# Storing the last block of a matrix product in pieces of 16, 8 and 8 rows, with two instead of six buffers for the transposed chunks

## Chip, cores, metric

One core of one Trainium2 chip. The metric is the device time of one execution in microseconds (us), as the median of several runs; less is better. PE is the engine for matrix products (PEld its loads of weights), DVE the vector engine, ACT the scalar engine, POOL the general one, and SP here only issues DMAs; SBUF and PSUM are the core's two memories on the chip. Every large DMA is spread over the core's sixteen DMA engines. The profile's span is about 1.8 us shorter than that time (165.4 against 167.18 us for the profiled run before).

## The reference

The reference builds a weight from a matrix, a low-rank product and a norm per column, and multiplies a large x by it. The weight is small; x and the result are 33.5 MB each.

```python
batch, seq_len, in_dim, out_dim = 16, 2048, 256, 256     # rank 16
W_adapted = W + scale * (lora_A @ lora_B)
W_final = W_adapted / np.sqrt(np.sum(W_adapted**2, axis=0, keepdims=True) + 1e-8) * m
y = x.reshape(-1, in_dim) @ W_final                       # 32768 x 256 by 256 x 256
```

## The kernel before

x is cut into 8 blocks of 4096 rows (4 MB), 32 rows per partition. A block is loaded by one DMA on SP's queue, worked on in 8 chunks of 4 rows per partition, overwritten in place with its result, and stored by one DMA on ACT's queue. A chunk goes through four steps: 8 transposes on PE into PSUM, a cast to bf16 on DVE (which moves it to SBUF), 8 products on PE, and a copy from PSUM back into the block on ACT. There are five block buffers, so loads 5, 6 and 7 wait for stores 0, 1 and 2. The order of the instructions on each engine is not the order of the source: the framework's scheduler picks it, and the number of buffers limits it.

```python
J = 4; DJ = 32; BLK = DJ * P; NBLK = N // BLK
xpool  = ctx.enter_context(tc.tile_pool(name="xpool", bufs=5))
xtpool = ctx.enter_context(tc.tile_pool(name="xtpool", bufs=6))
pp_xt  = ctx.enter_context(tc.tile_pool(name="pp_xt", bufs=2, space=bass.MemoryType.PSUM))
pp_y   = ctx.enter_context(tc.tile_pool(name="pp_y", bufs=2, space=bass.MemoryType.PSUM))
# ... (loads of the small inputs, w_final) ...
for b in range(NBLK):
    x_sb = load_x(b)                                   # one nc.sync.dma_start, 4 MB
    for c in range(DJ // J):
        xt_ps = pp_xt.tile([P, KC, J * P], FP32, tag="psxt", name="xt_ps")
        # ... 8 x nc.tensor.transpose into xt_ps ...
        xt_sb = xtpool.tile([P, KC, J * P], BF16, name="xt_sb")
        nc.vector.tensor_copy(out=xt_sb, in_=xt_ps)
        y_ps = pp_y.tile([P, J, OUT], FP32, tag="psy", name="y_ps")
        # ... 8 x nc.tensor.matmul of xt_sb with w_final into y_ps ...
        nc.scalar.copy(out=x_sb[:, c * J : (c + 1) * J, :], in_=y_ps)
    nc.scalar.dma_start(
        out=out_flat[b * BLK : (b + 1) * BLK].rearrange("(p j) k -> p j k", p=P),
        in_=x_sb)
```

Of the kernel before, what the change touches and what calls it, by code (L numbers as in the profile page):

```python
# [11 lines left out]
def kernel(  # L12
# [10 lines left out]
    nc = tc.nc  # L23
    P = 128
# [6 lines left out]
    out_flat = out.flatten_outer_dims()  # L31
# [4 lines left out]
    J = 4  # L36
    DJ = 32
    BLK = DJ * P
    NBLK = N // BLK
# [3 lines left out]
    consts = ctx.enter_context(tc.tile_pool(name="consts", bufs=1))  # L43
    startup = ctx.enter_context(tc.tile_pool(name="startup", bufs=1))
    xpool = ctx.enter_context(tc.tile_pool(name="xpool", bufs=5))
    xtpool = ctx.enter_context(tc.tile_pool(name="xtpool", bufs=6))
    pp_xt = ctx.enter_context(tc.tile_pool(name="pp_xt", bufs=2, space=bass.MemoryType.PSUM))
    pp_y = ctx.enter_context(tc.tile_pool(name="pp_y", bufs=2, space=bass.MemoryType.PSUM))

    def load_x(b):  # L50
        t = xpool.tile([P, DJ, IN], FP32, name="x_sb", tag="x_sb")
        nc.sync.dma_start(
            out=t,
            in_=x_flat[b * BLK : (b + 1) * BLK].rearrange("(p j) k -> p j k", p=P),
        )
        return t
# [23 lines left out]
    with tc.high_priority():  # L80
# [15 lines left out]
        for c in range(KC):  # L96
# [10 lines left out]
            out=wa, in0=ab_ps, scalar=float(scale), in1=w_nat, op0=ALU.mult, op1=ALU.add  # L107
# [21 lines left out]
    for a in range(J // 2):  # L129
        j_order.append(a)  # L130
        j_order.append(a + J // 2)

    for b in range(NBLK):
        x_sb = load_x(b)


        for c in range(DJ // J):
            xt_ps = pp_xt.tile([P, KC, J * P], FP32, tag="psxt", name="xt_ps")
            for j in range(J):
                for kc in range(KC):  # L140
                    nc.tensor.transpose(  # L141
                        xt_ps[:, kc, j * P : (j + 1) * P],
                        x_sb[:, c * J + j, kc * P : (kc + 1) * P],
                        identity,
# [5 lines that stand above are left out]
            for kc in range(KC):  # L150
                for j in j_order:
                    nc.tensor.matmul(  # L152
                        y_ps[:, j, :],
                        xt_sb[:, kc, j * P : (j + 1) * P],
                        w_final[:, kc, :],
                        start=(kc == 0 and (j % (J // 2)) == 0),
                        stop=(kc == KC - 1 and (j % (J // 2)) == (J // 2) - 1),
                    )
            nc.scalar.copy(out=x_sb[:, c * J : (c + 1) * J, :], in_=y_ps)  # L159

        nc.scalar.dma_start(
            out=out_flat[b * BLK : (b + 1) * BLK].rearrange("(p j) k -> p j k", p=P),
            in_=x_sb,
        )


# [33 lines left out]
```

## Time and profile before

| | before |
|---|---|
| median time, 4 runs (range) | 167.03 us (166.91 to 167.78) |
| span of the profiled run | 165.4 us |
| bytes moved | 67.55 MB |
| last copy of a result ends | 153.14 us |
| last store issued | 153.18 us |
| last data packet lands | 163.93 us |

From the page, the span in 40 slices of 4.1 us: busy tenths of PE and of the DMA queues, and the rate.

```profile
PE   0059588888999889988998999888998699797000
...
DMA  6999989899999989999999998989999999992885
GB/s 194 480 412 404 483 380 503 380 380 380 452 432 388 499 380 456 430 404 468 384 491 388 452 432 388 499 382 456 428 404 468 396 471 404 444 444 83 380 380 254
```

The one slice in which the DMA queues are mostly idle is the fourth from the end, where the rate is 83 GB/s. A slice books a packet where it starts, so single slices swing; longer stretches swing less. From the windows of the profile, with for each stretch its length, the busy time of the engines, the granted clock, the busy share of the DMA queues and the rate (x133 means 133 instructions):

```profile
core 0: us, PE busy (x) PEld busy (x) DVE busy (x) ACT busy (x) POOL busy (x), PEclk, DMA share, GB/s
128.00:146.00 18.00, 15.54 (x133) 13.30 (x132) 8.78 (x9) 9.02 (x9) 0.00 (x0) 1.00 1.00 429
...
149.00:151.50 2.50, 2.32 (x21) 1.87 (x20) 0.00 (x0) 2.29 (x3) 0.00 (x0) 1.00 0.33 138
151.50:154.00 2.50, 0.60 (x6) 0.29 (x3) 0.00 (x0) 1.44 (x2) 0.00 (x0) 1.00 0.00 0
154.00:159.00 5.00, 0.00 (x0) 0.00 (x0) 0.00 (x0) 0.00 (x0) 0.00 (x0) 0.59 1.15 492
```

The queues are full (429 GB/s) until about 149 us, start nothing between 151.5 and 154 us, and then work alone. The hole is the wait for the last copy. The timeline of ACT (start, duration, what, and in brackets the idle time before) shows the copy and the store that follows it:

```profile
150.00 1.93 ACT L159 COPY x_sb<-y_ps 128x1024 f32<-128x1024 f32 x2 [0.21 <-PE y_ps L152]
152.13 1.01 ACT L159 COPY x_sb<-y_ps 128x1024 f32<-128x1024 f32 x1 [0.21 <-PE y_ps L152]
153.18 0.34 ACTq L161 DMA_DIRECT2D out_dram<-x_sb  x1
```

The timeline of DVE, from block 0 to block 2, shows how six buffers are used: up to six casts in a row, then a long pause while PE makes the products that belong to them.

```profile
33.40 2.36 DVE L147 CAST xt_sb<-xt_ps 128x1024 bf16<-128x1024 f32 x2 [1.75 <-PE xt_ps L141]
37.51 7.18 DVE L147 CAST xt_sb<-xt_ps 128x1024 bf16<-128x1024 f32 x6 [1.76 <-PE xt_ps L141]
46.75 2.36 DVE L147 CAST xt_sb<-xt_ps 128x1024 bf16<-128x1024 f32 x2 [2.06 <-PE y_ps L152]
54.46 7.18 DVE L147 CAST xt_sb<-xt_ps 128x1024 bf16<-128x1024 f32 x6 [5.36 <-PE xt_ps L141]
```

The trace also holds each DMA packet's start, duration, queue and size. A store ends with one small record of completion per DMA engine; the sixteen of each store say when each of the sixteen engines was done. Sorted, in us:

```
store of block 6:  149.52 149.55 149.56 149.56 149.71 149.97 150.57 150.63 150.76 150.80 150.86 150.95 151.06 151.06 151.10 152.20
store of block 7:  163.76 163.77 163.78 163.78 163.79 163.79 163.81 163.83 163.83 163.84 163.85 163.86 163.87 163.88 163.89 163.92
```

One engine is 1.1 us behind the next and 2.7 us behind the first when block 6 ends. ("The slow engine" is this one of the sixteen.) Its 32 KB packets take 1.27 us in this stretch (18 of them from 129.47 to 152.21 us); 1.213 us is the usual duration, found in 1571 of the 2048. The trace does not name the engine of a packet: "this engine" means packets each of which starts when the one before ends. After the hole all sixteen start level and end level.

### The profile page before, as it was taken

The page shows a single profiled execution, that of the slowest core. Times are in us where ns is not written, and L with a number is a line of the kernel's source. Part 1 is how long each engine was busy: PE and PEld are TensorE (multiplying, and loading weights), DVE is VectorE, ACT ScalarE, POOL GpSimd, SP SyncE. Part 2 cuts the span into 40 slices and gives each one's busy share as a digit, 9 for nine tenths or more (in the row PEclk, how much of TensorE's full clock was granted, in tenths as well). Part 3 has the DMA queues.
Part 4 walks back from the last instruction along what each step waited for, and adds up shares of the span by engine and source line. Part 5 has one row for each costly group of instructions (what it writes and reads, how often), then busy time and mean ns, then how long its engine had stood idle before and what let it go on. Part 6 is the DMA issues. An engine that isn't in the chain of part 4 may idle for free.

```text
span 165.4 us, 2364 instructions
## 1 busy us (share of the span) xinstructions
PE 128.5 (78%) x1034; PEld 107.4 (65%) x1034; DVE 81.3 (49%) x76; ACT 65.6 (40%) x67; POOL 0.7 (0%) x6
## 2 busy tenths in 40 slices
PE   0059588888999889988998999888998699797000
PEld 0037577776788778876877778777786678685000
DVE  0155655559750885059553951577519350780000
ACT  3001244441068405960097039620780089329000
POOL 1000000000000000000000000000000000000000
PEclk9999999999999999999999999999999999999755
DMA  6999989899999989999999998989999999992885
GB/s 194 480 412 404 483 380 503 380 380 380 452 432 388 499 380 456 430 404 468 384 491 388 452 432 388 499 382 456 428 404 468 396 471 404 444 444 83 380 380 254
DMA packets 2892, 67.55 MB, mean 408 GB/s; under 512 B 561, under 2 KB 834, under 8 KB 834
## 3 DMA queue, kind: packets, MB, share of 16 engines
q1 hardware_dynamic: 1424, 33.82, 48.4%
q10 hardware_dynamic: 1458, 33.59, 47.4%
q8 instruction: 8, 0.13, 0.3%
q14 instruction: 2, 0.02, 0.0%
HBM read 33.85 MB, written 33.55 MB: 408 GB/s over the span
## 4 chain that ended last, share of the span: by engine, by line
PE 57%; DVE 23%; ACT 6%; DMA 4%; issue 2%; ACTq 1%
PE y_ps L152 32%; PE xt_ps L141 23%; DVE xt_sb L147 20%; ACT x_sb L159 6%; DMA m_row<-in_m_dram 4%; PE n_ps L115 1%; DVE rnorm L124 1%; PE mb_ps L91 1%; DVE w_final L126 0%; DVE sq L110 0%; DVE wa L106 0%; ACTq L60 0%; ACTq L64 0%; ACT norm L119 0%; PE ab_ps L97 0%
## 5 line engine op out<-in xcount | busy, mean ns | idle before, releaser
L147 DVE CAST xt_sb<-xt_ps 128x1024 bf16<-128x1024 f32 x64 | 75.6, 1220 | 55.7 <-PE xt_ps L141 41.8
L159 ACT COPY x_sb<-y_ps 128x1024 f32<-128x1024 f32 x64 | 63.6, 1014 | 75.1 <-PE y_ps L152 72.8
L141 PE MATMUL xt_ps<-identity,x_sb 128*128 128x128 f32 x512 | 70.6, 278 | 7.0 <-DVE xt_sb L147 6.4
L152 PE MATMUL y_ps<-w_final,xt_sb 128*128 128x256 bf16 x512 | 64.7, 272 | 6.9 <-DVE xt_sb L147 5.0
L141 PEld LDWEIGHTS xt_ps<-identity,x_sb 128*128 128x128 f32 x512 | 57.2, 142 | 15.8 <-DVE xt_sb L147 14.8
L152 PEld LDWEIGHTS <-xt_sb 128*128 128x128 bf16 x512 | 49.1, 97 | 17.4 <-DVE xt_sb L147 6.9
L119 ACT ACTIVATE norm<-n_ps,eps_col 128x256 f32<-128x256 f32 x1 | 0.5, 474 | 10.1 <-PE n_ps L115 10.1
L91 PE MATMUL mb_ps<-m_row,ones 1*128 1x256 f32 x2 | 1.2, 694 | 4.2 <-DMA m_row<-in_m_dram 4.2
L86 PE MATMUL aT_ps<-identity,a_nat 128*16 128x128 f32 x2 | 0.6, 396 | 3.9 <-DMA a_nat<-in_lora_A_dram 3.9
L91 PEld LDWEIGHTS mb_ps<-m_row,ones 1*128 1x128 f32 x2 | 0.5, 304 | 4.7 <-issue 4.7
L115 PE MATMUL n_ps<-sq,ones 128*128 128x256 f32 x4 | 2.1, 674 | 1.5 <-DVE sq L110 1.5
L82 DVE CAST b_bf<-b_nat 16x256 bf16<-16x256 f32 x1 | 0.3, 282 | 5.5 <-DMA b_nat<-in_lora_B_dram 5.5
L124 DVE RECIPROCAL rnorm<-norm 128x256 f32<-128x256 f32 x1 | 1.8, 1753 | 2.0 <-ACT norm L119 2.0
L86 PEld LDWEIGHTS aT_ps<-identity,a_nat 128*16 128x16 f32 x2 | 0.1, 88 | 3.9 <-issue 3.9
L115 PEld LDWEIGHTS n_ps<-sq,ones 128*128 128x128 f32 x4 | 1.2, 324 | 2.2 <-DVE sq L110 2.0
L76 ACT ACT_TABLE_LOAD x1 | 1.3, 1283 | 2.3 <-issue 2.3
L93 DVE COPY m_all<-mb_ps 128x256 f32<-128x256 f32 x1 | 0.4, 425 | 2.9 <-PE mb_ps L91 2.9
L126 DVE TENSOR_TENSOR w_final<-wam,rnorm 128x256 bf16<-128x256 f32 x2 | 0.8, 422 | 0.0
L122 DVE TENSOR_TENSOR wam<-wa,m_all 128x256 f32<-128x256 f32 x2 | 0.8, 416 | 0.0
L110 DVE TENSOR_TENSOR sq<-wa 128x512 f32<-128x512 f32 x1 | 0.7, 692 | 0.0
L106 DVE SCALAR_TENSOR_TENSOR wa<-ab_ps,w_nat 128x512 f32<-128x512 f32 x1 | 0.7, 692 | 0.0
L97 PE MATMUL ab_ps<-b_bf,aT 16*128 16x256 bf16 x2 | 0.6, 416 | 0.0
(11 smaller groups left out, 2.0 us busy)
## 6 DMA issues: line engine op xcount, KB each, us to landing
x_sb<-in_x_dram SPq DMA_DIRECT2D x8, 4096.0 KB, 32.5
out_dram<-x_sb ACTq DMA_DIRECT2D x8, 4096.0 KB, 25.0
w_nat<-in_W_dram SPq DMA_DIRECT2D x1, 256.0 KB, 2.9
a_nat<-in_lora_A_dram ACTq DMA_DIRECT2D x1, 16.0 KB, 3.1
b_nat<-in_lora_B_dram ACTq DMA_DIRECT2D x1, 16.0 KB, 5.2
m_row<-in_m_dram ACTq DMA_DIRECT2D x1, 1.0 KB
```

What stands on the lines that cost most here:

```text
L76: nc.scalar.activation(out=warm, in_=eps_col, func=AF.Sqrt)
L86: nc.tensor.transpose(aT_ps[:, c * P : (c + 1) * P], a_nat[:, c, :], identity)
L91: nc.tensor.matmul(mb_ps, ones[0:1, :], m_row, start=True, stop=True)
L106: nc.vector.scalar_tensor_tensor(out=wa, in0=ab_ps, scalar=float(scale), in1=w_nat, op0=ALU.mult, op1=ALU.add)
L115: nc.tensor.matmul(n2_ps, ones, sq[:, c, :], start=(c == 0), stop=(c == KC - 1))
L122: nc.vector.tensor_mul(out=wam[:, c], in0=wa[:, c], in1=m_all)
L124: nc.vector.reciprocal(out=rnorm, in_=norm)
L126: nc.vector.tensor_mul(out=w_final[:, c], in0=wam[:, c], in1=rnorm)
L141: nc.tensor.transpose(xt_ps[:, kc, j * P : (j + 1) * P], x_sb[:, c * J + j, kc * P : (kc + 1) * P], identity,)
L147: nc.vector.tensor_copy(out=xt_sb, in_=xt_ps)
L152: nc.tensor.matmul(y_ps[:, j, :], xt_sb[:, kc, j * P : (j + 1) * P], w_final[:, kc, :], start=(kc == 0 and (j % (J // 2)) == 0), stop=(kc ...
L159: nc.scalar.copy(out=x_sb[:, c * J : (c + 1) * J, :], in_=y_ps)
```

## The change

The first part keeps the transposes from running ahead of the products, so that a block's result is finished more evenly. The second lets the store of the last block begin after half of it is done, so that little is left to store after the last copy.

```diff
-    xtpool = ctx.enter_context(tc.tile_pool(name="xtpool", bufs=6))
+    xtpool = ctx.enter_context(tc.tile_pool(name="xtpool", bufs=2))
...
+    CH = DJ // J
+    store_after = [[CH] for _ in range(NBLK)]
+    store_after[-1] = [CH // 2, 3 * CH // 4, CH]
...
         x_sb = load_x(b)
+        j_stored = 0
...
             nc.scalar.copy(out=x_sb[:, c * J : (c + 1) * J, :], in_=y_ps)
-        nc.scalar.dma_start(
-            out=out_flat[b * BLK : (b + 1) * BLK].rearrange("(p j) k -> p j k", p=P),
-            in_=x_sb)
+            if c + 1 in store_after[b]:
+                j0 = j_stored
+                j_stored = (c + 1) * J
+                nc.scalar.dma_start(
+                    out=out_flat[b * BLK : (b + 1) * BLK].rearrange(
+                        "(p j) k -> p j k", p=P)[:, j0:j_stored, :],
+                    in_=x_sb[:, j0:j_stored, :])
```

More of the change, by code (lines that the diff above doesn't have):

```diff
@@ L159 @@
             nc.scalar.copy(out=x_sb[:, c * J : (c + 1) * J, :], in_=y_ps)
-        nc.scalar.dma_start(
-            out=out_flat[b * BLK : (b + 1) * BLK].rearrange("(p j) k -> p j k", p=P),
-            in_=x_sb,
-        )
+            if c + 1 in store_after[b]:
[3 more added lines that the diff above has]
+                    out=out_flat[b * BLK : (b + 1) * BLK].rearrange(
+                        "(p j) k -> p j k", p=P
+                    )[:, j0:j_stored, :],
+                    in_=x_sb[:, j0:j_stored, :],
+                )
 _INS = ['x', 'W', 'lora_A', 'lora_B', 'm', 'scale']
```

## The prediction

> **What bounds the kernel now.** By windows of 20 us, from 40 to 140 us the DMA queues move 428 to 434 GB/s. The Trainium skill, page "DMA: Bandwidth & Descriptors", section "Specifications", gives a fabric ceiling of 435 GB/s; this trace agrees (best stretch 434). 67.55 MB at 432 GB/s is 156 us of a 165.4 us span: the body is DMA-bound. Compute hardly waits for loads (0.6 us in the waits), but is nearly as long: chunks run from 17 to 153.1 us, 64 chunks at 2.13 us.
>
> The exception is the tail. The packet records show the store of block 6 running dry between 149.5 and 152.2 us, engine by engine; the timeline shows the last store issued at 153.18 us, after the last copy; its first packet moves at 154.02 us. Then 4.19 MB go alone until 163.93 us. The hole is about 3.7 us of all engines' time. The sixteen engines do not end together: fifteen end block 6 by 151.1 us, one at 152.21 us, because its 32 KB packets took about 1265 ns where the others took 1213. The hole hides that skew: after it all start level and end within 0.17 us.
>
> **What the change does.** Two buffers stop the transposes from running six chunks ahead. In the timeline, blocks 1 to 7 show bursts of six casts (DVE-limited, 1.22 us each) and then bursts of copies; block 0 shows a pair pattern, two transposes then two products, at 4.11 us a pair, which never has more than two transposed chunks alive. I expect that pattern throughout: 16.4 us a block instead of 17, the last copy at about 149 us.
>
> The split adds two DMA issues on ACT (0.34 us each) and makes the last packets 16 or 8 KB. The first 16 rows should be ready at about 141 us (148.9 us even in the old order), before the store queue runs dry at 149.5 us. So the hole closes, and the queues run without a break.
>
> **On the critical path.** Loads and earlier stores do not move: the stores are backlogged, so issuing them earlier changes nothing. What can be won is the hole only: 3.7 us on average over engines, but the end is that of the slowest engine. It ends block 6 at 152.21 us and then has 8 partitions of 32 KB, 9.75 us: 161.96 us instead of 163.93, a gain of 2.0 us; if its lag is smaller in unprofiled runs, up to 3.5 us. Smaller packets and two more completions should cost about 0.1 us (estimate from the 9 ns completion records). I predict 164.7 us; 163.4 to 165.7 should hold it 8 times in 10. Faster by over 2% (under 163.65): 0.2; within 2%: 0.78; slower: 0.02.
>
> **What would show it.** GB/s near 430 in all slices after 146 us; data ending at about 162 us, with a ragged finish of 1 to 2.5 us between engines; the last copy at 147 to 151 us; copies in pairs, 2.05 us a chunk, no burst of six casts; PE and DVE busy times unchanged; the first piece issued before 149 us; the chain of waits ending in DMA.
>
> **What would make it wrong.** An instruction order that with two buffers serialises transpose, cast and product (over 2.3 us a chunk): then block 6's store comes after the queue is dry (142 us) and the gain is lost or reversed. A smaller skew: over 2% faster. Small packets much slower than 32 KB ones: less gain.

## The result

| | before | after |
|---|---|---|
| median time, 4 runs each (range) | 167.03 us (166.91 to 167.78) | 165.17 us (165.07 to 165.55) |
| span of the profiled run | 165.4 us | 163.3 us |
| last copy ends | 153.14 us | 151.29 us |
| last store issued | 153.18 us | 151.33 us |
| last data packet lands | 163.93 us | 161.87 us |
| a block, from store issue to store issue | 17.0 us (blocks 0 to 7, mean) | 16.76 us |

The ratio is 0.988, with an interval of 0.985 to 0.992: within 2%, and clearly not nothing. A ratio here is the mean time of one kernel's fast runs over the mean of the other's of the same rounds, so it is not quite the ratio of the medians.

The slices of the page after: from the second slice on the DMA row stays at 8 or 9 until the last one, and the slice of 83 GB/s is gone.

```profile
PE   0049888888888888888888888898889888886000
...
DMA  6999998999999899999999999999999999999992
GB/s 197 414 474 401 449 450 381 474 425 377 389 425 474 385 470 425 387 482 409 421 466 393 458 429 393 492 393 421 474 401 441 429 409 466 409 413 429 407 425 86
```

The windows after, for the stretches shown of before: no stretch without DMA until 159 us, then a thin end.

```profile
core 0: us, PE busy (x) PEld busy (x) DVE busy (x) ACT busy (x) POOL busy (x), PEclk, DMA share, GB/s
128.00:146.00 18.00, 16.18 (x142) 14.22 (x140) 9.70 (x9) 8.96 (x9) 0.00 (x0) 1.00 0.99 426
...
149.00:151.50 2.50, 1.16 (x10) 0.70 (x8) 0.14 (x1) 2.02 (x2) 0.00 (x0) 1.00 0.95 406
151.50:154.00 2.50, 0.00 (x0) 0.00 (x0) 0.00 (x0) 0.00 (x0) 0.00 (x0) 1.00 1.04 446
154.00:159.00 5.00, 0.00 (x0) 0.00 (x0) 0.00 (x0) 0.00 (x0) 0.00 (x0) 0.56 0.95 401
159.00:162.00 3.00, 0.00 (x0) 0.00 (x0) 0.00 (x0) 0.00 (x0) 0.00 (x0) 0.50 0.36 150
```

The timeline of ACT after: the three pieces are issued at 145.05, 149.16 and 151.33 us.

```profile
145.05 0.34 ACTq L170 DMA_DIRECT2D out_dram<-x_sb  x1
...
149.16 0.34 ACTq L170 DMA_DIRECT2D out_dram<-x_sb  x1
150.28 1.01 ACT L165 COPY x_sb<-y_ps 128x1024 f32<-128x1024 f32 x1
151.33 0.34 ACTq L170 DMA_DIRECT2D out_dram<-x_sb  x1
```

The timeline of DVE after: never more than two casts in a row, in all eight blocks.

```profile
33.61 2.35 DVE L153 CAST xt_sb<-xt_ps 128x1024 bf16<-128x1024 f32 x2 [1.76 <-PE xt_ps L147]
37.72 2.36 DVE L153 CAST xt_sb<-xt_ps 128x1024 bf16<-128x1024 f32 x2 [1.76 <-PE xt_ps L147]
42.14 2.36 DVE L153 CAST xt_sb<-xt_ps 128x1024 bf16<-128x1024 f32 x2 [2.06 <-PE y_ps L158]
46.25 2.36 DVE L153 CAST xt_sb<-xt_ps 128x1024 bf16<-128x1024 f32 x2 [1.76 <-PE xt_ps L147]
```

And the completion records of the sixteen engines, from the packets of the trace:

```
store of block 6:  149.35 149.38 149.44 149.54 149.69 150.22 150.28 150.61 150.73 150.77 150.85 150.88 150.90 150.92 150.94 152.10
last piece:        159.12 159.15 159.20 159.31 159.46 159.99 160.05 160.38 160.50 160.54 160.62 160.65 160.67 160.68 160.70 161.86
```

(The slow engine's record of the piece before, 159.41 us, falls between them and is left out.) The store of block 6 ends where it ended before, engine by engine. The slow engine is done with block 6 at 152.10 us, and then has 8 packets of 16 KB (607 ns each, 4.86 us) and 16 of 8 KB (306 ns each, 4.90 us): 152.10 + 4.86 + 4.90 = 161.86 us, to the hundredth what was recorded. Fifteen engines are done by 160.70 us.

### The profile page after: what moved, and what is told of

It reads as the page before. It is cut to its first block, busy times and chain, and to the rows that moved or that the text cites. A ratio compares the mean times of both kernels' runs of the same rounds, so it can differ in the third digit from the quotient of the medians.

```text
span 163.3 us, 2370 instructions
## 1 busy us (share of the span) xinstructions
PE 125.4 (77%) x1034; PEld 107.9 (66%) x1034; DVE 81.1 (50%) x76; ACT 66.1 (40%) x67; POOL 0.7 (0%) x6
## 4 chain that ended last, share of the span: by engine, by line
PE 57%; DVE 26%; DMA 4%; issue 2%; ACT 1%; DVEq 1%; ACTq 1%
PE y_ps L158 33%; DVE xt_sb L153 23%; PE xt_ps L147 22%; DMA m_row<-in_m_dram 4%; PE n_ps L115 1%; DVE rnorm L124 1%; DVEq L206 1%; PE mb_ps L91 1%; ACT x_sb L165 1%; DVE w_final L126 0%; DVE sq L110 0%; DVE wa L106 0%; ACTq L60 0%; ACTq L64 0%; ACT norm L119 0%
## 5 line engine op out<-in xcount | busy, mean ns | idle before, releaser
L158 PE MATMUL y_ps<-w_final,xt_sb 128*128 128x256 bf16 x512 | 65.5, 273 | 11.5 <-DVE xt_sb L153 11.5
L147 PE MATMUL xt_ps<-identity,x_sb 128*128 128x128 f32 x512 | 68.7, 279 | 3.4 <-DVE xt_sb L153 3.1
L147 PEld LDWEIGHTS xt_ps<-identity,x_sb 128*128 128x128 f32 x512 | 58.7, 144 | 7.8 <-DVE xt_sb L153 6.7
L158 PEld LDWEIGHTS <-xt_sb 128*128 128x128 bf16 x512 | 47.8, 98 | 22.8 <-DVE xt_sb L153 18.2
```

What stands on the lines that cost most here:

```text
L147: nc.tensor.transpose(xt_ps[:, kc, j * P : (j + 1) * P], x_sb[:, c * J + j, kc * P : (kc + 1) * P], identity,)
L158: nc.tensor.matmul(y_ps[:, j, :], xt_sb[:, kc, j * P : (j + 1) * P], w_final[:, kc, :], start=(kc == 0 and (j % (J // 2)) == 0), stop=(kc ...
```

## The experiments

Theories, as they stood before the runs. **A**: the DMA queues set the end, and among the sixteen engines the slowest one: the change is worth just the idle time that this one engine had in the hole, 1.8 us (152.20 to 154.03 us), and not the 3.6 us that the engines had on average (mean start 154.08 less mean end 150.50 us; the prediction says 3.7). **B**: the instruction order earned it; the last copy came 1.85 us earlier and the time fell by 1.86 us, so the numbers of the result alone cannot tell B from A. **C**: the split earned it. **D**: no single engine matters, all sixteen share one rate and the bytes set the end.

| run | median us (range) | ratio to before, interval | last store issued | data end |
|---|---|---|---|---|
| the whole change | 165.17 (165.07 to 165.55) | 0.988 (0.985 to 0.992) | 151.33 | 161.87 |
| e1: split alone | 165.61 (165.16 to 166.97) | 0.990 (0.986 to 0.995) | 153.68 | 162.09 |
| e2: two buffers alone | 165.38 (165.31 to 165.45) | 0.987 (0.983 to 0.992) | 151.38 | 162.13 |
| e3: two pieces of 16 rows | 165.25 (165.13 to 165.28) | 0.987 (0.983 to 0.990) | 151.07 | 161.97 |
| e4: last piece as 120 + 8 partitions | 165.46 (165.30 to 166.09) | 0.989 (0.985 to 0.992) | 151.42 | 162.43 |
| e5: no PE work (wrong) | 162.86 (162.73 to 162.96) | 0.972 (0.967 to 0.977) | 147.58 | 159.85 |
| e6: last stores on SP's queue | 165.17 (164.95 to 165.32) | 0.986 (0.982 to 0.989) | 151.49 | 162.12 |
| e7: four buffers alone | 165.96 (165.06 to 166.94) | 0.990 (0.986 to 0.995) | 151.00 | 161.76 |
| e8: last piece as 80 + 35 + 13 | 166.52 (166.08 to 166.81) | 0.996 (0.994 to 0.998) | 150.98 | 163.01 |
| e9: no PE work, but casts (wrong) | 163.30 (163.24 to 163.57) | 0.977 (0.974 to 0.980) | 145.02 | 160.23 |

Issue and data end are of the profiled run of each kernel; in e4 and e8, where the last piece is two or three DMAs, the issue is that of the first. The kernel before, run beside them, had medians of 167.33, 167.47 and 167.32 us over 11, 11 and 12 runs; one run of each was slow and is left out of the ratios. The edits are given against the changed kernel, shortened where "..." or a comment stands. "Time" in the texts is the median; "queue" in them means one of the sixteen DMA engines' queues.

### e1, the split alone

```diff
-    xtpool = ... bufs=2
+    xtpool = ... bufs=6
```

> Six buffers, last block in three pieces (the split alone). Theory A (the end is set by the slowest DMA queue, busy without a break): the first piece is issued at about 148.9 us, when most queues are about to run dry and the slowest still has 3 us of work, so the data end at about 162 us and the time is 165.2 us (165.0 to 165.6), as with the whole change, although the last copy stays at 153.1 us. Theory B (the instruction order earns it: the last copy came 1.85 us earlier, 151.3 instead of 153.1 us, and the time fell by 1.86 us): this kernel keeps the old order and stays at 166.6 to 167.0 us.

Measured 165.61 us. Here the last copy is even later than before, 153.65 us, because the issues of the first two pieces (0.34 us each) stand between the copies; the data end at 162.09 us all the same. B, as the only cause, falls: the old order with the split earns nearly all of the gain. The timeline of ACT shows the pieces:

```profile
149.00 0.34 ACTq L170 DMA_DIRECT2D out_dram<-x_sb  x1
...
151.34 0.34 ACTq L170 DMA_DIRECT2D out_dram<-x_sb  x1
...
153.68 0.34 ACTq L170 DMA_DIRECT2D out_dram<-x_sb  x1
```

The first piece comes just in time (149.00 us, when the first engines run dry at 149.65 us). The windows show the hole nearly closed:

```profile
149.00:151.50 2.50, 2.08 (x18) 1.67 (x18) 0.00 (x0) 1.93 (x2) 0.00 (x0) 1.00 0.82 341
151.50:154.00 2.50, 0.90 (x8) 0.56 (x6) 0.00 (x0) 1.93 (x2) 0.00 (x0) 1.00 0.98 419
```

Two of the six runs were slower, 166.65 and 166.97 us. They left no trace, so what made them slower stays open.

### e2, two buffers alone

```diff
-    store_after[-1] = [CH // 2, 3 * CH // 4, CH]
```

> Two buffers, last block stored whole (the order alone). Theory A: the hole in the DMA stays but is shorter, the last store is issued at about 151.3 us, its first packets move at 152.1 us on all queues together, and 9.9 us later, at 162.0 us, the data end level (spread under 0.3 us): 165.2 us (165.0 to 165.6). So each part alone would earn nearly all, and the two together no more. Theory B: 165.2 us too. Theory C (the split earns it all): 167.0 us.

Measured 165.38 us, data end 162.13 us, with the sixteen engines level within 0.15 us (161.97 to 162.12). C, as the only cause, falls. This is the run that is most worth looking at, because the hole is still there. Its windows, and the issue of its one store of the last block:

```profile
146.00:149.00 3.00, 2.55 (x24) 2.13 (x21) 2.16 (x2) 1.12 (x2) 0.00 (x0) 1.00 0.89 382
149.00:151.50 2.50, 1.22 (x10) 0.70 (x8) 0.20 (x1) 2.02 (x2) 0.00 (x0) 1.00 0.34 144
151.50:154.00 2.50, 0.00 (x0) 0.00 (x0) 0.00 (x0) 0.00 (x0) 0.00 (x0) 0.85 0.98 419
...
151.38 0.34 ACTq L169 DMA_DIRECT2D out_dram<-x_sb  x1
```

Fifteen engines run dry between 149.2 and 151.2 us and are idle until about 152.2 us, and it costs next to nothing, because the slow engine is busy with block 6 until 152.05 us, and the last store, issued at 151.38 us, reaches the engines at about 152.2 us. The whole change closes this hole for the fifteen too, and its data end only 0.26 us earlier (161.87 us): idle time of fifteen engines was next to free as long as the sixteenth had almost none.

By itself e2 cannot tell A from B. Its store is issued 1.80 us earlier than before, and its data end 1.80 us earlier; that this shift is just the idle time of the slow engine (1.8 us) is chance.

So each half of the change earns almost the whole gain, and the two together no more: 1.7 us (e1, by medians), 1.95 us (e2) and 1.86 us (both).

### e3, two pieces of 16 rows

```diff
-    store_after[-1] = [CH // 2, 3 * CH // 4, CH]
+    store_after[-1] = [CH // 2, CH]
```

> Two buffers, last block in two pieces of 16 rows. Theory A: the last piece is issued at about 151.3 us while the queues have work until 154.2 us, so the third piece is not needed: 165.2 us, within 0.2 us of the whole change, with the same ragged end. Rival (a small last piece shortens the tail): 165.7 us or more.

Measured 165.25 us, data end 161.97 us, with the slow engine last again (161.96 us, the others by 161.17 us). The third piece earns nothing: the second of two pieces is issued at 151.07 us, and the engines have work until 154.24 us.

### e4, one engine without a share of the last piece

```diff
-                nc.scalar.dma_start(out=...[:, j0:j_stored, :], in_=x_sb[:, j0:j_stored, :])
+                # last piece only: cuts = [0, P - 8, P], else [0, P]
+                for p0, p1 in zip(cuts[:-1], cuts[1:]):
+                    nc.scalar.dma_start(out=...[p0:p1, j0:j_stored, :], in_=x_sb[p0:p1, j0:j_stored, :])
```

> The whole change, but the last piece of 8 rows goes as two DMAs: partitions 0 to 119 (15 queues of 8 partitions) and 120 to 127 (8 queues of one partition), so that one of the sixteen queues has nothing of the last piece. Theory A, if the slowest queue is the one left out: its 8 packets of 306 ns are gone, the others get 0.3 us at most, the data end at about 161.0 us instead of 161.9: 164.3 us (164.0 to 164.6). If the slowest is another queue: 165.1 to 165.6 us, and the page of the packets tells whether it carried 8 or 9 of them. Theory D (all queues share one rate, 432 GB/s, and the raggedness is noise): 165.2 us.

Measured 165.46 us. This run rests on a statement of the Trainium skill, page "DMA: Bandwidth & Descriptors", section "Why a DMA increments its semaphore by 16 and not by 1": a DMA from SP or ACT uses the lowest-numbered k engines, k being the largest number up to 16 that divides the slowest dimension of both sides. The trace agrees in that the 120-partition piece left 15 completion records and the 8-partition piece 8. The slow engine finished its 8 packets of the first of these DMAs at 161.79 us and a ninth at 162.10 us, so the engine left out was another one, and the guess that the slow one is the last of the sixteen was wrong. A second engine ended later still, at 162.43 us: from 156.9 to 160.2 us eleven 8 KB packets took 334 to 1169 ns instead of the usual 309. Why is not shown. As a test of A against D this run does not decide.

### e5, the same traffic without PE

```diff
-            # transposes, cast, products, copy from y_ps
+            t = xtpool.tile([P, J, IN], FP32, name="xt_sb")
+            nc.scalar.copy(out=t, in_=x_sb[:, c * J : (c + 1) * J, :])
+            nc.scalar.copy(out=x_sb[:, c * J : (c + 1) * J, :], in_=t)
```

> Wrong result on purpose: loads, stores, pieces and buffers as in the whole change, but each chunk is only copied twice by ACT (about 2 us a chunk, so that the stores come at about the same rate); no transposes, products or casts. Theory A with the slow queue tied to the work of the engines: no queue has store packets of 1255 to 1280 ns any more, the data end at 160.2 us (159.7 to 160.7) and the time is 163.6 us (163.0 to 164.0). Theory A with a queue that is slow by itself: the packets of about 1260 ns stay, the data end at 161.5 us or later, 165.0 us. Theory D (no slow queue matters, the bytes and one rate set the end): 165.2 us.

The result is x itself, so it is wrong. Measured 162.86 us, a little under the range that I gave. From 130 to 150 us only one packet of 1235 to 1330 ns is left (in the whole change there is an unbroken row of them on one engine), and the sixteen engines end between 159.17 and 159.84 us. The loads and stores are the same bytes in the same pieces, and D, which has no place for an end that depends on PE's work, fails here. But such packets are not gone from the whole run: from 68 to 125 us there are 22 of them, as many as in the whole change in that stretch, many of them 2.45 us apart, as a load and a store of one engine would be. So they come without PE's work too. The eight fetches of 16 KB of instructions, 0.9 us each, are gone too, which is worth about 0.46 us per engine on average (8 x 0.93 / 16, an estimate from their durations). Of the 2.0 us by which the data end earlier, 0.9 us is what all the others gained (160.70 to 159.84 us), about half of it explained by those fetches; the other 1.2 us is the lag of the slow engine.

### e6, the last three blocks' stores on SP's queue

```diff
-                nc.scalar.dma_start(
+                (nc.sync if b >= NBLK - 3 else nc.scalar).dma_start(
```

> The whole change, but the stores of the last three blocks are issued by SP, on the queue that carried the loads. If the slow packets belong to the queue of ACT (only stores showed them, 1258 ns, while loads on the same engines took 1213), they vanish for 12 MB of the stores, the lag shrinks by up to 1 us and the time is 164.2 to 164.8 us. If they belong to stores as such, or to one DMA engine while the others work, the time stays at 165.2 us (165.0 to 165.5).

Measured 165.17 us, as the whole change. The page shows the traffic moved:

```profile
q1 hardware_dynamic: 2144, 46.40, 66.8%
q10 hardware_dynamic: 1026, 21.01, 30.0%
```

The row of packets of 1236 to 1284 ns moved with the stores to q1, and the slow engine again ended last, at 162.11 us, the others by 161.07 us. The slowness belongs neither to a queue nor to the engine that issues.

### e7, four buffers alone

```diff
-    xtpool = ... bufs=2
+    xtpool = ... bufs=4
-    store_after[-1] = [CH // 2, 3 * CH // 4, CH]
```

> Four buffers, last block stored whole. The last store is issued with the last copy, whose time the order sets: if the bursts of casts shorten with the buffers, at 152 to 152.7 us, between the 151.4 us of two buffers and the 153.2 us of six. Theory A then says data end = issue + 0.8 + 9.9 us, level: 163.0 us and 166.2 us of time (165.7 to 166.6), because this issue comes after the slowest queue has run dry at 152.1 us. Theory C (only the split counts): 167.0 us.

My guess of the order was wrong: the last store is issued at 151.00 us, earlier than with two buffers. The rule held: 151.00 + 0.8 + 9.9 = 161.7 us, and the data ended at 161.76 us, level within 0.15 us. The profiled run took 165.06 us; the six runs spread up to 166.94 us, and the slower ones left no trace. So how early the last copy comes does not fall steadily with the number of buffers.

### e8, more for the low engines, less for the rest

```diff
+                # last piece only: cuts = [0, 80, 115, P]
```

> The whole change, but the last piece of 8 rows goes as three DMAs of 80, 35 and 13 partitions. If a DMA of n partitions runs on as many of the lowest-numbered queues as divide n (16, 7 and 13), queues 0 to 6 get 11 packets of 306 ns instead of 8, queues 7 to 12 get 6 and 13 to 15 get 5. The run with 120 and 8 partitions showed the slowest queue with a packet of the 8-partition piece, so it is one of 0 to 7. If it is queue 7 (the Trainium skill, page DMA: Bandwidth & Descriptors, section Latency and other measured facts, names engines 7 and 15 as usually slower): it ends 0.6 us earlier, queues 0 to 6 end 0.9 us later, the data end at 161.3 to 161.6 us and the time is 164.6 to 165.0 us. If it is one of 0 to 6: its 3 extra packets come at the very end, the data end at 162.8 us and the time is 166.0 us (165.7 to 166.3).

Measured 166.52 us, data end 163.01 us: the case in which the slow engine is one of 0 to 6. The slow engine's three completion records of the last piece say so themselves. It has done the second piece at about 159.6 us; then come 5 packets (record at 161.15 us), 5 more (162.69 us), and one (163.00 us), 11 packets of 306 ns where the whole change gave it 8. (The three DMAs left 36 completion records in all, which is 16 + 7 + 13 as my text has it; that they take the lowest-numbered engines rests on the rule cited at e4 and is not shown by the trace.) The total bytes are the same: by the rule seven engines had three small packets more and the other nine two or three fewer, and the slow one, among the seven, ended last, 0.65 us after the next (162.36 us). Beside the whole change that is 1.14 us of data end and 1.35 us of median (on different chips); three packets of 306 ns are 0.92 us. This is A seen directly, and D falls: the same bytes took longer. Engine 7, which my text had as a candidate, it is not. (e4 and e8 ran on different chips, so their slow engines need not be the same.)

### e9, casts but no PE

```diff
-            t = xtpool.tile([P, J, IN], FP32, name="xt_sb")
-            nc.scalar.copy(out=t, in_=x_sb[:, c * J : (c + 1) * J, :])
-            nc.scalar.copy(out=x_sb[:, c * J : (c + 1) * J, :], in_=t)
+            t = xtpool.tile([P, J, IN], BF16, name="xt_sb")
+            nc.vector.tensor_copy(out=t, in_=x_sb[:, c * J : (c + 1) * J, :])
+            u = xtpool.tile([P, J, IN], FP32, name="u_sb")
+            nc.scalar.copy(out=u, in_=t)
+            nc.scalar.copy(out=x_sb[:, c * J : (c + 1) * J, :], in_=u)
```

> Wrong result on purpose: as the run without PE, but DVE casts each chunk to bf16 and ACT copies it twice. If the slow packets come from the work of PE (its instructions or its reads), they stay away as before and the time stays at 162.9 us (162.5 to 163.3). If DVE's casts bring them, a queue with packets of 1255 to 1280 ns is there again and the time is 164 us or more.

Measured 163.30 us, the upper edge of what I gave; wrong result. DVE casts 64 chunks again (from SBUF, 0.69 us each instead of 1.22), and still there are only two packets of 1235 to 1330 ns in the whole stretch from 70 to 150 us. So these casts and copies do not bring the slow engine. What both runs left out is PE's work, the reads of PSUM that follow it and the fetches of instructions, and both have no slow row in the last 20 us of stores. That any of these is the cause is not shown: e5 had 22 such packets before 125 us without them. Two engines ended 0.6 us after the others (160.11 and 160.22 us), for which I have no reason.

No run points to a version that beats the whole change clearly. e2, e3 and e6 lie within 0.2 us of it.

## Why the prediction was right

It gave 164.7 us, from 163.4 to 165.7, and within 2%; 165.17 us was measured. Its own sum, a gain of 2.0 us, makes 165.0; the 164.7 leaned towards a smaller lag, which did not come.

- **The body is DMA-bound, stores are backlogged, earlier issues change nothing.** Right: the store of block 6 ended at 149.5 to 152.2 us before and 149.4 to 152.1 us after, although it was issued 4.3 us earlier (134.64 instead of 138.91 us).
- **The hole closes, but only the slowest engine's idle time is won: 161.96 us instead of 163.93.** Right: 161.87 us. e2 beside the whole change, and e8, show it from both sides: idle time of the other engines was nearly free, and extra packets on the slow one were paid in full.
- **Small packets cost about 0.1 us.** Right, as far as it can be seen: the slow engine took 4.86 + 4.90 = 9.76 us for its share of the last block, where the prediction reckoned 9.75 us with whole packets.
- **If the lag were smaller in unprofiled runs, up to 3.5 us.** The gain was 1.86 us by medians, 2.06 us by the profiles' data ends. Whether the lag is smaller without the profile's recording is open, as no run was made without it.
- **The pair pattern throughout, 16.4 us a block, last copy at 149 us.** Partly: casts do come in pairs only, but once per block ACT waits 3.95 us and a block takes 16.76 us, so the last copy ended at 151.29 us. It cost nothing, since the piece that follows it was not waited for: that piece was issued at 151.33 us, and no engine was done with the first piece before 154.2 us.
- **PE busy time unchanged.** It fell from 128.5 to 125.4 us, with the same 1034 products and transposes. **The chain of waits ending in DMA.** The chain follows instructions, and both chains end at the last copy. **A ragged finish of 1 to 2.5 us.** The first engine was done at about 159.1 us, the last at 161.87.
- What the prediction did not see: that the two halves of the change do the same thing twice. It reckoned the earlier last copy and the split as steps to one end, and did not ask what each is worth alone.

Open: what slows store packets on one engine by 4%. In the last 20 us of stores it went with PE's work in all nine kernels that have it and was absent in the two without (one and two such packets), but e5 shows like packets earlier without PE. The recording of the profile cannot be ruled out, as no run here was made without it. Open, too, why kernels with six or four buffers now and then take 1 to 2 us more (e1, e7), while two buffers with the whole-partition pieces (the change, e2, e3, e6) stayed within 164.95 to 165.55 us.

## What to carry to other kernels

In this DMA-bound kernel, a hole in the DMA row near the end was worth the idle time of the slowest of the engines, not the mean: look at when each one finishes, and ask how long that one stands idle. Two repairs of the same hole did not add up; try each alone before keeping both. Once the last store went out early enough for the queues not to run dry, a further cut of it earned nothing (e3).

## What the Trainium skill lacked or had wrong

- "DMA: Bandwidth & Descriptors", section "Specifications", gives an HBM limit of about 358 GB/s per core without a condition; the note in the page's section "Bandwidth" adds that it is for both cores of an HBM domain streaming. The row is thus incomplete, not wrong. This program, on one core, moved 431 GB/s, reads and writes together, from 41 to 146 us, which is near the fabric ceiling of 435 GB/s of the same table.
- The same page, section "Latency and other measured facts", has engines 7 and 15 as usually slower, with a cause (a best guess) that is tied to DMAs issued from GpSimd; here only SP and ACT issue. In e8 the slow engine was one of 0 to 6 (by the page's own rule of which engines a DMA takes, and the records of e8 at 161.15, 162.69 and 163.00 us), and its lag is that of 1.27 us for a stored 32 KB packet against 1.213 us (before); with PE's work left out the sixteen ended within 0.7 us (e5), 1.2 us in e9.
- "Perfetto Trace Analysis", section "DMA Optimizations", says that splitting DMAs may let some start sooner if the engines are idle. That agrees (e1). It lacks that the gain is that of the slowest engine: the engines were idle for 3.6 us on average, and 1.86 us were won. (The nearest to it is on the page "DMA: Bandwidth & Descriptors", section "iDMA fabric", in an explanation marked as unconfirmed: a bulk load runs at the pace of its slowest engine.)
